# Nine small edits to the order and the buffers of a hybrid mLSTM and MLA block on one core

## The chip, the cores and the metric

The kernel runs on one core of a Trainium2 chip. The metric is the device time of one execution in microseconds (us), the median of three runs. A core has five engines that each work through an instruction queue of their own, in order: PE (TensorE, matrix products; its weight loads stand under PEld), DVE (VectorE), ACT (ScalarE), POOL (GpSimd) and SP (SyncE), which in this kernel issues all the DMAs. Semaphores hold an instruction, and with it its whole queue, until what it needs is there.

## The reference

One layer of an encoder over 2048 tokens of width 1024, all in fp32:

```python
xn = rms_norm(h, ln_mix_g);  proj = xn @ w_in
y_a = mlstm_group(q, k, v, o, gates)      # 4 heads of 128, forward and backward, in chunks of 128
y_b = mla_group(c_q, c_kv, k_rope, ...)   # 4 heads, softmax over all 2048 keys
h = h + concat(y_a, y_b) @ w_out
h = h + conv_gated_mlp(rms_norm(h))       # 2816 wide, centred convolution of 3 taps
h = h + sigmoid(rms_norm(h) @ w_ple_gate) * rms_norm(p @ w_ple_proj)
out = rms_norm(h, final_g)
```

## The kernel before, in words

Every fp32 operand of a large product is split into a high part (ACT copies it, L121) and a low part (DVE subtracts, L124), and three products of the parts are added in PSUM. Large matrices go through a Strassen-like scheme: block sums T1 to T4, B11, B21, B22 of the moving operand, sums S1 to S4 and A11 to A22 of the stationary one, seven products for a pair of column tiles.

The stages, with their time in the profiled execution:

- **Input projection** (`in_proj`, L187, 0 to 193 us). Sixteen row groups of 128 tokens. A group `st` has a product for the small columns (`nat(st, wr)`, 24 matmuls of 464), the transposes of the group before (`turn_rest`), and a product for the values (`vals`, 24 matmuls of 512). Beside them the rows' norm factors are computed (`square`: ACT squares a row tile, POOL takes the power -0.5, L144) into `rcol`. `norm_row` (L296) transposes eight columns of `rcol` on PE, and stores them to DRAM (`r_d`); `token_sums` (L398) loads them back as a broadcast (`rrow`) and forms the scaled block sums, which it stores in `xo_d` or splits at once. `norm_row` is called at groups 3 and 5, ahead of the group's product. `pair_begin` (L493) starts the next stage's first weights.
- **Pairs** (`pairs`, L503, 193 to 429 us). Twelve pairs of column tiles, seven products of 12 matmuls each. `begin` queues operands that are loaded from `xo_d` into four tiles t0 to t3 in turn; `load` splits one into place and lets the next be loaded. T3 of the first half is the first in this queue. `side(at)` runs small work between two products, and in it the generator `gates` (L870) takes a step at every second call.
- **Queries** (`queries`, L750, 429 to 495 us). Eight blocks `c` of 256 tokens: `rope(c)`, `turn(c - 1)`, `latent(c)`, with stores of the queries to `q_d`. `split_c` splits the raw latents of a block into w10 or w2 in turn. `attend_begin` (L1136) is a generator whose steps start the attention: it loads the first two query pairs (L1195, L1196) and splits the first (L1197), then scores the first tile, then takes exponentials. It is made at `c == 4`. The split query parts lie in u2 (the very first in w2).
- **Attention and mLSTM** (`attend`, L1210, 495 to 1201 us). 64 tiles (4 heads by 16), each with a written order of scores `s`, transposes `t`, exponentials `E`, value products `V`, and 13 dots. At a dot `pump` adds `rate` to a counter, and for every whole unit it takes one step of the generator `mlstm` (L979): `rate = SIDE / (64 * 13)`. The steps of `mlstm` go backward over the chunks (133 steps) and then forward (497 steps). In a forward chunk the keys are loaded from `kn_d` into w12 (`kk`, L1065, L1069), weighted (L999), and multiplied into the state (L1006); the values get a column of ones by a memset per chunk (L988); the heads' outputs `hy` are scaled by norm factors (L1125, pinned) and transposed on PE (L1130), `pause(n)` letting n dots' worth of steps go by.
- **Stream** (`stream`, L1681, 1201 to 2857 us): output projection, gated MLP, embedding gate. `opening` (L1345), stepped in the last attention tiles, loads its first weights-to-be (`yr`, from `y_d`) and their row factors (`rb`), and `Out.scale` (L1958) multiplies them (L1960).

What orders the work: the library's planner lays out each engine's queue. It takes the trace order as priority, but lets an instruction pass that it estimates to be ready earlier, so a load or a copy can stand in its queue well ahead of its place in the code (the row loads of `mlstm` at L1034 are issued at 433.23 us, amid the queries). `keep_in_program_order` pins an instruction behind all that was traced before it on its engine, and `manual_schedule` keeps an engine's whole queue in trace order, as for PE in `queries`. A tile of a tag (`self.at(tag, ...)`) takes the place of the tag's last one, and is written when all readers of that one are done.

Of the kernel before, what the change touches and what calls it, by code (L numbers as in the profile page):

```python
# [34 lines left out]
EPS = 1e-6  # L35
SB = 512
LAG_T, LAG_X, LAG_R = 1, 2, 2
SIDE = 678
KSCALE = 128.0 ** -0.5
ASCALE = 192.0 ** -0.5  # L40

# [7 lines left out]
def _f(ap):  # L49
    return ap.bitcast(F32)  # L50
# [10 lines left out]
class Block:  # L61
# [125 lines left out]
    def in_proj(self):  # L187
# [108 lines left out]
        def norm_row(blk):  # L296
            ps = self.tbank([8, P])
            nc.tensor.transpose(ps, rcol[:, 8 * blk:8 * blk + 8], self.ident)
            o = self.at(next(srot), [8, P], name="r8")
            nc.scalar.copy(o, ps)  # L300
            nc.sync.dma_start(self.r_d.rearrange("(t p) -> t p", p=P)[8 * blk:8 * blk + 8], o)
# [38 lines left out]
        for st in range(2, NT):  # L340
            if st == 4:
                pc = self.tbank([P, 36])
                nc.tensor.transpose(pc, cw, self.ident[:36, :36])
                self.taps = self.cst.tile([P, 4, 2 * NC2], F32, name="fcw")
                self.edge = self.cst.tile([P, 2 * NC2, 2], F32, name="edge")
                self.cwt = self.taps.rearrange("p a c -> p (a c)")[:, 0:36]
                nc.vector.tensor_copy(self.cwt, pc)
            if st in (3, 5):
                norm_row(st // 2 - 1)
            if st == 7:  # L350
                self.pair_load(0)
            if st + 2 < NT:
                load_x(st + 2)
            if st + 1 < NT:
                split_x(st + 1)
            rest(st, nat(st, wr, NREST))
            if st < 5:
                for q in range(4 * st - 4, 4 * st):
                    square(q)
            if st > 3:  # L360
                next(work, None)
            if st < NT - 1:
                turn_rest(st - 1)
            if st == NT - 2:
                continue
            if st == NT - 1:
                vals(st - 1)
                finish(st - 1)
                finish(st)
                turn_rest(st - 1)  # L370
            if st > 3:
                next(work, None)
            vals(st)
            if st < NT - 1:
                finish(st)
            if st > 3:
                next(work, None)
# [115 lines left out]
    def pair_begin(self):  # L493

        self.PAIRS, self.npair = (("w3", "w4"), ("x11",), ("w5", "w6"), ("w8", "w9"), ("x10",)), -1
        self.pair_load(1)
        self.begun = self.pair_prep(0)
        next(self.begun)
        yield
        next(self.begun)  # L500
        yield

    def pairs(self):  # L503
# [89 lines left out]
        class Pair:  # L593
            pass

        begin(0, ("T3", "T4", "B22"))
        gates, prev = self.gates(), None
        for i in range(12):
            blk, j = divmod(i, 6)
            then = i == 5  # L600
            s = Pair()
            s.i, s.pr, s.blk, s.ops = i, j, blk, self.ops.pop(i)
            x, s.y = [self.pfa.tile([P, SB], F32, name=t, tag=t) for t in ("fx", "fy")]
            s.z, s.spare = [self.pfb.tile([P, SB], F32, name=t, tag=t) for t in ("fz", "fs")]
            s.u = [None, None]

            def side(at):
                if i == 0 and at == 1:
                    next(self.begun)
                if i == 0 and at in (2, 3):  # L610
                    load("T3", range(2))
                if i == 0 and at in (5, 6):
                    load("T4", range(2))
                if i == 1 and at in (1, 2):
                    load("B22", range(2))
                if (1, 4) < (i, at) < (5, 0) and at % 2:
                    self.gate_bank = prev.spare if at % 2 else s.spare
                    next(gates, None)
                if i == 11:
                    self.queries_begin(at, prev.spare if at % 2 else s.spare)  # L620

            if i < 2:
                op = self.xop["B11"][0]
                nc.tensor.matmul(s.y, s.ops["A11"][0][:, 0:P], op[0], start=True, stop=True)
            prod(x, s.ops["A11"], "B11")
            nc.scalar.copy(s.y, x)
            if then:
                load("B11")
            side(1)
            prod(s.z, s.ops["S1"], "T1")  # L630
            s.p5 = self.at("t6", [P, SB], name="p5")
            nc.scalar.copy(s.p5, s.z)
            if then:
                load("T1")
            side(2)
            if prev:
                rest_y(prev)
            if i == 6:
                load("T4")
            side(3)  # L640
            prod(s.y, s.ops["S2"], "T2", True)
            s.u[0] = self.at(next(urot), [P, 2 * SB + 2], name="ug")
            nc.scalar.copy(s.u[0][:, 1 + SB:1 + 2 * SB], s.y)
            if then:
                load("T2")
            side(4)
            if i + 1 < 12:
                for _ in self.pair_prep(i + 1):
                    pass
            if i + 2 < 12:  # L650
                self.pair_load(i + 2)
            if i == 10:
                self.queries_load()
            prod(x, s.ops["A12"], "B21", True)
            first_half(s, 0, x)
            side(5)
            if prev:
                rest_z(prev)
            if i == 6:
                load("B22")  # L660
            side(6)
            if then:
                load("B21")
            prod(s.y, s.ops["S3"], "T3", True)
            s.u[1] = self.at(next(urot), [P, 2 * SB + 2], name="uv")
            add(s.u[1][:, 1 + SB:1 + 2 * SB], s.p5, s.y)
            if then:
                load("T3")
            side(7)
            if i == 4:  # L670
                begin(1, self.NAMES)
            prev = s
            if i == 4:
                assert next(gates, 0) == 0
            if i == 10:
                nc.scalar.activation(part, part, AF.Silu)
                nc.sync.dma_start(self.qk_d[7, :, :, P - 1], part)
# [72 lines left out]
    def queries(self):  # L750
# [76 lines left out]
        with self.tc.manual_schedule(engines={mybir.EngineType.PE}):  # L827
# [7 lines left out]
            for c in range(8):  # L835
# [8 lines left out]
                    kr = self.split_latent(1, ("x14", "x15"), (c - 1, c), None if c == 1 else kr)  # L844
                if c in (4, 5, 6, 7):
                    vv = self.split_latent(2, ("x10", "x11"), (c - 4,), None if c == 4 else vv)
                if 0 < c < 7:
                    split_c(c + 1)
                if c == 3:
                    self.tc.keep_in_program_order(nc.scalar.activation(self.stat(1, "warm"), self.nhalf[:, 0:1], AF.Exp))  # L850
# [1 line left out]
                    turn(c - 1)  # L852
                latent(c, 0)
                latent(c, 1)
                if c == 4:
                    self.kr2, self.krl = kr
                    att = self.attend_begin()
                    next(att)
                if c > 4:
                    next(att, None)  # L860
        self.vh, self.vl = vv
        self.last_block = lambda: turn(7)
# [7 lines left out]
    def gates(self):  # L870
# [69 lines left out]
        o = tl()  # L940
        flip(o, b)
        yield
        pt = pbank()[:, 0:16]
        nc.tensor.matmul(pt, selt, ms[:, 0:16], start=True, stop=True)
        mp, nml, so = col("mp"), col("nml"), col("so")
# [33 lines left out]
    def mlstm(self):  # L979
# [2 lines left out]
        hc = lambda n, r, j: self.cols[n].rearrange("p (r c h) -> p r c h", r=2, h=NH)[:, r, j]  # L982
        mbank = lambda s: self.pml.tile(s, F32, name="mb", tag="ml")

        def load_v(c):
            v1 = self.at(f"t{c % 2}", [P, NH, 129], name="v1")
            nc.sync.dma_start(v1[:, :, 0:P], self.v_d[c].rearrange("p (h e) -> p h e", h=NH))
            nc.vector.memset(v1[:, :, P:129], 1.0)  # L988
            return v1

        def turn_k(kn, kT):
            pk = mbank([P, NH, P])
# [62 lines left out]
        for c in range(NT):  # L1055
# [6 lines left out]
            og = self.at("t6", [P, NH, P], name="og")  # L1062
            nc.sync.dma_start(og, self.o_d[c])
            if c < NT - 1:
                kk = self.at("w12", [P, 2, NH, P], name="kk")  # L1065
                if c == 0:
                    turn_k(kk[:, 0], qk[:, 4:8, :])
                else:
                    nc.sync.dma_start(kk[:, 0], self.kn_d[c])  # L1069
# [51 lines left out]
            for h in range(NH):  # L1121
                nc.scalar.activation(hy[:, 1, h, :], hh[:, h, :], AF.Square, accum_out=ssq[:, h:h + 1])
            r4 = self.rsq(ssq, NH, 1.0 / P)
            yield from pause(2)
            a = nc.vector.tensor_tensor(hh, hh, r4.unsqueeze(2).broadcast_to([P, NH, P]), op=ALU.mult)  # L1125
            self.tc.keep_in_program_order(a)
            yield from pause(3)
# [8 lines left out]
    def attend_begin(self):  # L1136
# [4 lines left out]
        rsums = self.gt.rearrange("p a b -> p (a b)")  # L1141

        def load_q(h, pr):
            q = self.at(f"w{4 - pr % 2}", [P, 2, 256], F32R, "q_t")
            nc.sync.dma_start(_f(q), self.q_d[h, pr])
            qv[h, pr] = q

        def split_q(h, pr):

            q = qv[h, pr]  # L1150
            qs = self.at("u2" if (h, pr) != (0, 0) else "w2", [P, 2, 256], F32R, "q_s")
            self.split(_f(q[:, 0]), qs[:, 0], qs[:, 1])
            qv[h, pr] = qs[:, 0], qs[:, 1], q[:, 1]

        class Tile:
            pass
# [37 lines left out]
        self.steps = load_q, split_q, score_bank, start, soft, expo, rowsum  # L1194
        load_q(0, 0)  # L1195
        load_q(0, 1)  # L1196
        split_q(0, 0)  # L1197
        yield
        self.first = cur = start(0, 0)
# [734 lines left out]
class Out:  # L1934
# [22 lines left out]

    def scale(self, i, e):  # L1958
        a = self.b.raw[i][e][:, 4:8].rearrange("p h t -> p (h t)")
        self.nc.vector.tensor_tensor(a, a, self.rb[e], op=ALU.mult)  # L1960

    def load_x(self, i, e):
        c = self.tile(i, e)
# [372 lines left out]
```

## Time and profile before

| | us |
|---|---|
| median of 3 runs | 2856.83 |
| lowest, highest | 2855.85, 2857.14 |
| the profiled execution | 2859.16 |
| its span, first to last instruction | 2857.4 |

| engine | busy us | share of the span |
|---|---|---|
| PE | 2816.5 | 99% |
| PEld | 2363.5 | 83% |
| DVE | 2131.6 | 75% |
| ACT | 1581.6 | 55% |
| POOL | 211.1 | 7% |

The mean granted TensorE clock is 0.996. A row of the timeline has the start in us, the duration, the engine, the line (L12 is line 12 of the kernel), the operation with out<-in, the shapes, the count, and in brackets the engine's idle time before it with what ended it. A row of the waits has a waiter, what released it, the total in us, the number of times and the longest. A row of the windows has the stretch, its length, PE's busy time (and count), the mean granted clock as a share, the share of time that the DMA engines were busy, and GB/s.

### The profile page before, as it was taken

What the parts mean: (1) busy time and instruction counts of PE and PEld (TensorE: products, weight loads), DVE (VectorE), ACT (ScalarE), POOL (GpSimd) and SP (SyncE); (2) the same over time, 40 slices, a digit from 0 to 9 for tenths busy, and PEclk for the clock granted to TensorE, in tenths of its full rate; (3) what the DMA queues carried; (4) which work ended last, traced back from release to release, by engine and by line L of the source; (5) the groups of instructions that cost most, each with busy time, mean ns of one, the idle gap of its engine ahead of it and who ended that gap; (6) DMA issues with size and microseconds to landing.
All of it is one profiled execution on the core that took longest, in us unless ns stands there. A gap on an engine that the chain in (4) does not pass through costs nothing.

```text
span 2857.4 us, 39996 instructions
## 1 busy us (share of the span) xinstructions
PE 2816.5 (99%) x13932; PEld 2363.5 (83%) x13932; DVE 2131.6 (75%) x3702; ACT 1581.6 (55%) x3072; POOL 211.1 (7%) x331
## 2 busy tenths in 40 slices
PE   8999998999999999999999999999999999999998
PEld 7888887888888888888888888888888888888787
DVE  4877766777887777877778787777778767676787
ACT  6346765555566566655655556655556333254655
POOL 2100000000000000044200000000000000011012
PEclk9999999999999999999999999999999999999999
DMA  8883758554443333578735544667776757575864
GB/s 281 288 250 113 214 161 243 159 172 128 130 131 116 99 112 107 156 244 276 254 134 199 176 169 162 199 199 229 238 237 209 236 192 237 171 266 200 287 202 163
DMA packets 444531, 552.73 MB, mean 193 GB/s; under 512 B 34564, under 2 KB 296744, under 8 KB 444328
## 3 DMA queue, kind: packets, MB, share of 16 engines
q1 hardware_dynamic: 444328, 550.16, 60.1%
q8 instruction: 110, 1.80, 0.3%
q14 instruction: 93, 0.76, 0.1%
HBM read 357.45 MB, written 192.61 MB: 193 GB/s over the span
## 4 chain that ended last, share of the span: by engine, by line
PE 84%; DVE 4%; DMA 3%; ACT 2%; issue 1%; POOL 0%; SPq 0%; POOLq 0%; ACTq 0%; DVEq 0%
PE fy L1700 22%; PE fz L1700 15%; PE fx L1700 14%; PE ppv L1239 4%; PE tb L1227 3%; PE fy L541 3%; PE fz L541 2%; PE ppv L1240 2%; PE bk L1163 2%; PE bk L1165 2%; PE bk L1166 2%; PE bk L1164 2%; PE bk L1167 2%; PE fx L541 2%; PE fs L134 2%; PE mb L1101 1%
## 5 line engine op out<-in xcount | busy, mean ns | idle before, releaser
L1700 PE MATMUL fz<-op,fw 128*128 128x512 f32 x1968 | 479.3, 392 | 3.8 <-ACT fw L121 3.8
L1700 PE MATMUL fx<-op,fw 128*128 128x512 f32 x1968 | 476.0, 390 | 0.0
L1700 PE MATMUL fy<-op,fw 128*128 128x512 f32 x1968 | 475.2, 390 | 0.0
L1700 PEld LDWEIGHTS fz<-op,fw 128*128 128x128 f32 x1968 | 368.5, 188 | 81.9 <-ACT fw L121 5.0
L1700 PEld LDWEIGHTS fy<-op,fw 128*128 128x128 f32 x1968 | 368.7, 188 | 77.0 <-DVE fh L1685 0.5
L1700 PEld LDWEIGHTS fx<-op,fw 128*128 128x128 f32 x1968 | 368.4, 188 | 75.9
L121 ACT CAST pt<-tb 128x512 fp32r<-128x512 f32 x256 | 147.5, 586 | 187.9 <-PE tb L1227 187.0
L1700 PE MATMUL fy<-op,fwd 128*128 128x512 f32 (+1 forms) x984 | 238.1, 390 | 0.0
L1168 DVE TENSOR_REDUCE mx<-bk 128x1 f32<-128x512 f32 x256 | 175.4, 686 | 67.2 <-PE bk L1167 64.8
L1700 PEld LDWEIGHTS fy<-op,fwd 128*128 128x128 f32 x984 | 182.9, 188 | 37.7 <-DVE uv L1685 0.4
L124 DVE TENSOR_TENSOR pt<-tb,pt 128x512 fp32r<-128x512 f32 x256 | 173.5, 686 | 33.4 <-ACT pt L121 32.7
L1239 PE MATMUL ppv<-pt,kv 128*128 128x512 f32 x512 | 188.6, 407 | 1.0 <-DVE pt L124 1.0
L1185 ACT ACTIVATE pe<-bk,nm 128x512 f32<-128x512 f32 x256 | 174.7, 698 | 21.2 <-DVE nm L1179 21.1
L124 DVE TENSOR_TENSOR fw<-fwr,fw 128x1024 fp32r<-128x1024 f32 x124 | 150.9, 1221 | 34.0 <-ACT fw L121 32.7
L121 ACT CAST op<-opr 128x512 fp32r<-128x512 f32 x205 | 120.7, 620 | 81.2 <-DMA opr<-xo_d 16.6
L124 DVE TENSOR_TENSOR op<-opr,op 128x512 fp32r<-128x512 f32 x205 | 134.6, 690 | 25.7 <-ACT op L121 25.5
L1227 PE MATMUL tb<-ident,pe 128*128 128x128 f32 x1024 | 150.5, 273 | 1.5 <-DVE pt L124 1.3
L121 ACT CAST fw<-fwr 128x1024 fp32r<-128x1024 f32 x124 | 129.7, 1051 | 37.3 <-DVE fwr L1674 21.3
L1240 PE MATMUL ppv<-pt,kv 128*128 128x256 f32 x512 | 144.2, 282 | 0.0
L1227 PEld LDWEIGHTS tb<-ident,pe 128*128 128x128 f32 x1024 | 122.2, 141 | 20.4 <-DVE pt L124 4.1
L121 ACT CAST fw<-hraw 128x1024 fp32r<-128x1024 f32 (+1 forms) x72 | 70.2, 980 | 115.8 <-PE fx L1700 58.8
L1748 DVE SCALAR_TENSOR_TENSOR fgv<-uv,fcw,fgv 128x1024 f32<-128x1024 f32 x88 | 112.8, 1282 | 16.0 <-ACT fgv L1746 9.5
(407 smaller groups left out, 5210.1 us busy)
## 6 DMA issues: line engine op xcount, KB each, us to landing
fwr<-in_w_up SPq DMA_DIRECT2D x66, 512.0 KB
fh<-h_d SPq DMA_DIRECT2D x48, 512.0 KB
h_d<-fh SPq DMA_DIRECT2D x48, 512.0 KB
s_d<-fwr SPq DMA_DIRECT2D x44, 512.0 KB
fws<-s_d SPq DMA_DIRECT2D x44, 512.0 KB
rw<-row_d SPq DMA_DIRECT2D x32, 512.0 KB
tw_d<-tsum SPq DMA_DIRECT2D x60, 256.0 KB
opr<-tw_d SPq DMA_DIRECT2D x60, 256.0 KB
```

The source lines that it names most:

```text
L121: nc.scalar.copy(hi, src)
L124: (sub or nc.vector).tensor_tensor(lo, src, _f(hi), op=ALU.subtract)
L134: mm = lambda *a, **k: self.nc.tensor.matmul(*a, **k, skip_group_check=more)
L541: nc.tensor.matmul(out, a[:, k * P:(k + 1) * P], parts[lo], start=first, stop=lo == 1 and k == 3, skip_group_check=more)
L1163: mm(ps, ql, kh[:, ks], start=True, stop=False)
L1168: nc.vector.tensor_reduce(s.mx[:, kb:kb + 1], ps, axis=AX.X, op=ALU.max)
L1185: nc.scalar.activation(s.pe[:, kb % 2], s.banks[kb], AF.Exp, bias=s.nm, accum_out=s.rs[:, kb:kb + 1])
L1227: nc.tensor.transpose(t[:, j, :], s.p[kb][:, j * P:(j + 1) * P], self.ident)
L1239: mm(w.ps, vh[:, ks], pts[kb][:, j], start=kt == 0, stop=False, skip_group_check=True)
L1240: mm(w.ps[:, 0], vl[:, ks], pts[kb][:, j, 0], start=False, stop=kt == NT - 1, skip_group_check=True)
L1700: nc.tensor.matmul(out, a[:, k * P:(k + 1) * P], parts[lo][:, cols], start=first, stop=lo == 1 and k == last, skip_group_check=more)
L1748: nc.vector.scalar_tensor_tensor(t, u[:, tap:tap + 2 * SB], self.taps[:, tap, ct:ct + 1], t, op0=ALU.mult, op1=ALU.add)
```

## The change

1. `norm_row` is called after the group's `turn_rest`, not before its product.
2. `pair_begin` loads T3 of the first half into w12 and w13 straight away; `pairs` splits it from there, and its queue starts with T4.
3. `gates` has one more `yield` ahead of the product with `selt`, so everything from there on comes one step later.
4. `attend_begin` is made at `c == 3`; a new `yield` separates the loads from the split. The steps are: loads after block 3, split after block 4, first scores after block 5 as before, exponentials after block 6.
5. The split query parts lie in the second half of the query's own tile (w3 or w4); `split_c(7)` is traced at the end of block 5 and not in block 6.
6. The forward keys take w12 and w13 in turn.
7. The tiles of values are made once, with their ones.
8. One more pause ahead of L1125 in each of 16 chunks; `SIDE` goes from 678 to 695.
9. The two calls of `Out.scale` for the first pair are pinned.

```diff
-SIDE = 678
+SIDE = 695
...
-            if st in (3, 5):
-                norm_row(st // 2 - 1)
             if st == 7:
...
                 turn_rest(st - 1)
+            if st in (3, 5):
+                norm_row(st // 2 - 1)
...
+        self.third = [self.at(t, [P, 2, SB], name="xt3") for t in ("w12", "w13")]
+        for k in range(4):
+            self.nc.sync.dma_start(self.third[k // 2][:, k % 2], self.xo_d[0, self.NAMES.index("T3"), k])
         self.pair_load(1)
...
-        begin(0, ("T3", "T4", "B22"))
+        begin(0, ("T4", "B22"))
...
                 if i == 0 and at in (2, 3):
-                    load("T3", range(2))
+                    for k in (2 * at - 4, 2 * at - 3):
+                        self.xop["T3"][k] = self.in_place(0, "T3", k)
+                        self.split(self.third[at - 2][:, k % 2], *self.xop["T3"][k])
...
-                if 0 < c < 7:
+                if 0 < c < 6:
                     split_c(c + 1)
...
-                if c == 4:
+                if c == 3:
                     self.kr2, self.krl = kr
                     att = self.attend_begin()
-                    next(att)
-                if c > 4:
+                if c == 5:
+                    split_c(7)
+                if c > 2:
                     next(att, None)
...
         flip(o, b)
+        yield
         yield
...
+        values = [self.at(f"t{e}", [P, NH, 129], name="v1") for e in range(2)]
+        for v1 in values:
+            nc.vector.memset(v1[:, :, P:129], 1.0)
+
         def load_v(c):
-            v1 = self.at(f"t{c % 2}", [P, NH, 129], name="v1")
-            nc.sync.dma_start(v1[:, :, 0:P], self.v_d[c].rearrange("p (h e) -> p h e", h=NH))
-            nc.vector.memset(v1[:, :, P:129], 1.0)
-            return v1
+            nc.sync.dma_start(values[c % 2][:, :, 0:P], self.v_d[c].rearrange("p (h e) -> p h e", h=NH))
+            return values[c % 2]
...
-                kk = self.at("w12", [P, 2, NH, P], name="kk")
+                kk = self.at(("w12", "w13")[c % 2], [P, 2, NH, P], name="kk")
...
-            yield from pause(2)
+            yield from pause(3)
             a = nc.vector.tensor_tensor(hh, hh, r4.unsqueeze(2).broadcast_to([P, NH, P]), op=ALU.mult)
...
-            q = self.at(f"w{4 - pr % 2}", [P, 2, 256], F32R, "q_t")
-            nc.sync.dma_start(_f(q), self.q_d[h, pr])
+            q = self.at(f"w{4 - pr % 2}", [P, 4, 256], F32R, "q_t")
+            nc.sync.dma_start(_f(q[:, 0:2]), self.q_d[h, pr])
...
-            qs = self.at("u2" if (h, pr) != (0, 0) else "w2", [P, 2, 256], F32R, "q_s")
-            self.split(_f(q[:, 0]), qs[:, 0], qs[:, 1])
-            qv[h, pr] = qs[:, 0], qs[:, 1], q[:, 1]
+            self.split(_f(q[:, 0]), q[:, 2], q[:, 3])
+            qv[h, pr] = q[:, 2], q[:, 3], q[:, 1]
...
         load_q(0, 1)
+        yield
         split_q(0, 0)
...
+        if i == -8:
+            self.b.tc.keep_in_program_order(a)
```

2 lines of the change are left out of this document (1 added, 1 removed).

## The prediction, as it was put on record

> **What bounds the kernel now.** I read the page first, then who waited for whom on PE, then the granted clock by stretches, then the timeline around each long wait.
>
> ```profile
> span 2857.4 us, 39996 instructions
> PE 2816.5 (99%) x13932; PEld 2363.5 (83%) x13932; DVE 2131.6 (75%) x3702; ACT 1581.6 (55%) x3072; POOL 211.1 (7%) x331
> ```
>
> PE is busy for all but 40.9 of 2857.4 us, and no other engine passes 75%. The change takes no matmul away. So it can win only what PE stands idle, and what PE runs slowly.
>
> ```profile
> PE bk L1163 <- DVE q_s L124: 6.8, 1, 6.8
> PE tb L298 <- POOL rcol L144: 4.5, 2, 2.6
> ...
> PE mb L1130 <- DVE hy L1125: 2.2, 3, 1.0
> PE mb L1130 <- DVE v L988: 1.9, 1, 1.9
> PE fy L541 <- ACT ug L643: 1.6, 1, 1.6
> PE qpr L134 <- DVE nm L1179: 1.6, 1, 1.6
> ...
> PE fs L944 <- DVE ms L939: 0.7, 1, 0.7
> ```
>
> These are the rows of PE's waits that the edits aim at, 19.3 us together. The slow running is in the clock; the columns are the stretch, its length, PE's busy time, the granted clock as a share, the DMA share and GB/s.
>
> ```profile
> 20.00:60.00 40.00, 37.41 (x176) 1.00 0.84 266
> ...
> 70.00:78.00 8.00, 7.62 (x32) 0.79 0.82 302
> ...
> 470.00:476.70 6.70, 6.50 (x20) 0.68 0.84 246
> ...
> 696.00:704.00 8.00, 6.11 (x30) 0.79 0.45 124
> ```
>
> Behind three of the idle stretches the clock is down, and behind the one of 2.59 us (in the first row) it is not. The price can be read from the same 24 matmuls with a full clock and a low one:
>
> ```profile
> 57.20 5.30 PE L134 MATMUL bk<-wsr,xh 128*128 128x464 f32 x24
> ...
> 70.40 6.83 PE L134 MATMUL bk<-wsr,xh 128*128 128x464 f32 x24
> ```
>
> The low clock cost 6.83 - 5.30 = 1.53 us, 0.91 of the 8 x 0.21 = 1.68 that the first window gives. The same share of the others makes 0.91 x 6.7 x 0.32 = 1.95 at 470 us and 1.53 at 698 us.
>
> **The change part by part.** Each sum is against the profiled execution (2859.16 us).
>
> *The rows' factors.*
>
> ```profile
> 45.47 0.55 POOL L144 TENSOR_TENSOR rcol<-rsm,nhalf 128x1 f32<-128x1 f32 x1
> ...
> 46.07 0.27 PE L298 MATMUL tb<-ident,rcol 128*8 128x128 f32 x1 [2.59 <-POOL rcol L144]
> ...
> 51.01 0.60 PE L283 MATMUL rtp<-ident,nn 128*128 128x128 f32 x4
> ...
> 66.46 0.33 SPq L148 DMA_DIRECT2D rrow<-r_d  x1
> ...
> 69.77 0.55 POOL L144 TENSOR_TENSOR rcol<-rsm,nhalf 128x1 f32<-128x1 f32 x1
> ...
> 70.38 0.27 PE L298 MATMUL tb<-ident,rcol 128*8 128x128 f32 x1 [1.96 <-POOL rcol L144]
> ...
> 86.50 1.23 DVE L124 TENSOR_TENSOR xh<-x_t,xh 128x1024 fp32r<-128x1024 f32 x1
> ...
> 93.93 2.26 PE L134 MATMUL bk<-wsr,xh 128*128 128x464 f32 x10
> ```
>
> The transposes stand ahead of a group's product and wait for POOL's last factor. Put behind the next transposes (51.01 less the 2.59 saved, so 48.4; the other at 70.38 - 1.96 - 2.59 + 5.30 = 71.1), they come when the factors are there (46.02 and 70.32, each 0.55 after its row). This takes away 2.59 + 1.96 and the 1.53 of clock: **6.08**. Their copy and store move along, past a row-tile load and some stores in SP's queue; the first reader is the broadcast at 66.46, 15 us on, so the move costs nothing unless it is delayed to there. What is late next? PE arrives 6.1 us earlier at each group, while row loads and token sums keep their DMA time. The tightest use I find is the split of 86.50, ready at 87.7 for the product at 93.93, which would then begin at 87.8: just enough even if DVE doesn't move up at all.
>
> *T3 sooner.*
>
> ```profile
> 179.48 1.06 SPq L469 DMA_DIRECT2D fwr<-in_w_in  x2
> ...
> 197.78 8.13 SPq L518 DMA_DIRECT2D opr<-xo_d  x5
> ...
> 204.22 1.27 ACT L121 CAST op<-opr 128x512 fp32r<-128x512 f32 x2 [3.72 <-DMA opr<-xo_d]
> ...
> 206.04 3.01 PE L541 MATMUL fy<-op,fw 128*128 128x512 f32 x12 [1.58 <-ACT ug L643]
> ```
>
> ACT stands 3.72 us at the split of an operand still on its way, the copy that PE needs is queued behind it, and PE waits 1.58. With T3 loaded some 20 us earlier this goes: **1.58**. The four loads now go through SP's queue ahead of 179.48, at 0.4 to 0.6 us each some 2 us; behind them stand the weights of the next pairs, which PE wants after 193. The weights of pair 2 (179.48) lose their place in w12 and w13 and must wait until T3 is split, at about 200. Twelve matmuls take some 2.7 us, and pair 2 begins eight such products after 206.04, at 228, or 220 if all before it is won. So this costs nothing; without that cover it would cost one load, 3.86 us by the row of the queries below.
>
> *The gates a step later.* The wait of 0.7 goes (**0.68**): DVE gets two products more, 5.4 us, before PE asks. All that follows is one step later too; the generator has 14 slots for 12 steps, and its results are read after the queries, 200 us on. So nothing waits for it.
>
> *The first queries.*
>
> ```profile
> 459.42 0.60 SPq L811 DMA_DIRECT2D q_d<-qo  x1
> ...
> 465.40 1.54 SPq L1145 DMA_DIRECT2D q_t<-q_d  x2
> ...
> 470.20 0.80 PE L1163 MATMUL bk<-kv,q_s 128*128 128x512 f32 x1 [6.82 <-DVE q_s L124]
> ```
>
> The chain of waits has the load's own time:
>
> ```profile
> 465.40 3.86 DMA q_t<-q_d
> ```
>
> PE is done with block 5 at 470.20 - 6.82 = 463.38 and waits for store, load, split. The loads are behind block 4's store in SP's queue, with no wait of their own: their place in the trace holds them. Traced a block earlier they come behind the store of 459.42. So issue at 460.02, landing 3.86 later at 463.88, and to the first score the 0.94 that it takes now (469.26 to 470.20): 464.8. ACT may be at the copies of block 5 then; I add 0.2. A wait of 1.6 is left of 6.82, and the clock's 1.95 goes with the rest: 6.82 + 1.95 - 1.6 = **7.17**. If the load lands at once, 8.77; if ACT, in order, puts the split behind the copy and the load takes twice as long, 7.17 - 3.86 = 3.3. The two issues push the next stores of SP by 1.0, which nothing on PE reads.
>
> *Block 7.*
>
> ```profile
> 486.32 0.62 ACT L121 CAST cq<-qraw 128x512 fp32r<-128x512 f32 x1 [4.02 <-PE bk L1167]
> ```
>
> The split of block 7 waits for the readers of the query parts in w2, and PE's rope product waits 1.58 for it. With the parts in the query's own tile, w2 is free when block 5 is done: **1.58**.
>
> *Keys in two places, ones once.*
>
> ```profile
> 690.81 0.38 SPq L1069 DMA_DIRECT2D kk<-kn_d  x1
> ...
> 696.28 0.69 DVE L999 SCALAR_TENSOR_TENSOR kk<-kk,cols 128x512 f32<-128x512 f32 x1 [3.34 <-DMA kk<-kn_d]
> ...
> 698.30 0.66 PE L1130 MATMUL mb<-ident,hy 128*128 128x128 f32 x4 [1.89 <-DVE v L988]
> ```
>
> One place for the keys means that the load waits for the state products of the chunk before; DVE then stands 3.34 us at the weighting, and the scaling that PE's transposes need is queued behind. With two places the load is a chunk early: 1.89 and its clock 1.53, **3.42**. The memsets that go are off the path: nothing.
>
> *A pause more, and the pin.*
>
> ```profile
> 1130.75 0.44 PE L1130 MATMUL mb<-ident,hy 128*128 128x128 f32 x2 [0.80 <-DVE hy L1125]
> ...
> 1155.70 0.69 DVE L1960 TENSOR_TENSOR yr<-yr,rb 128x512 f32<-128x512 f32 x1 [2.70 <-DMA rb<-ri_d]
> ...
> 1158.58 0.66 PE L1130 MATMUL mb<-ident,hy 128*128 128x128 f32 x4 [0.97 <-DVE hy L1125]
> ...
> 1170.10 0.66 PE L1227 MATMUL tb<-ident,pe 128*128 128x128 f32 x4 [0.56 <-DVE pt L124]
> ```
>
> The transposes' group by its tile shows the chunks:
>
> ```profile
> L1130 PE MATMUL mb<-ident,hy x64: 270/273/330, 663.2 to 1159.0; 128*128 128x128 f32 x64
> ```
>
> Sixteen chunks of four, 15 periods of 31 steps in 1159.0 - 663.2 us: a step is 1.07 us. The pause moves the transposes by that much, more than the 0.80 and the 0.4 that is left of the row of 2.2: **1.19**. DVE's 2.70 us at a broadcast that hasn't landed makes the 0.97, and I put the 0.56 down to the second scaling. Pinned, the scalings come in their place some ten us later, when it has landed. But what depends on them is pushed into the last two tiles; I keep half of 1.53: **0.77**, between 1.53 and -1.5 (one more wait like the present one).
>
> The rate goes from 0.815 to 0.835 steps a dot and the generator from 630 to 646 steps, so it ends as far before tile 60 as now (5.6 steps). But every step falls elsewhere between PE's matmuls. For new waits of this kind I subtract two of 0.97: **-1.94**.
>
> Sum: 6.08 + 1.58 + 0.68 + 7.17 + 1.58 + 3.42 + 1.19 + 0.77 - 1.94 = 20.5. The profiled execution would take 2838.6. It lies 2.33 above the median of the runs shown, so I forecast **2836.3** for the median.
>
> **The rivals.**
>
> *The first queries stay late* (0.13). For it: the DMAs are busy there (a share of 0.84 from 470), and stores of queries stand ahead of the load. Against it: the load waited for nothing. Price 5.2, which would leave 2.0 of 7.17: 2841.5. It decides if the load lands after 466.
>
> *The order does not do what the edit says* (0.08): the planner puts the factors' transposes ahead of the product again. For it: the copy of 204.22 and the scaling of 1155.70 stand in their queues ahead of work that was ready. Against it: the transposes before are pinned. It costs the 6.08: 2842.4.
>
> *Short gaps cost no clock* (0.05). Then 1.53 and 1.53 were not theirs and come back elsewhere: 20.5 - 3.1 = 17.4, so 2839.4. The rows of 70 and 696 us, with gaps of 1.96 and 1.89 ahead of them, speak against it; the row of 20 us, with 2.59, speaks for it. [...]
>
> *The steps fall badly* (0.08). There is one set of transposes (L1130) in each of 16 forward chunks, and now four of them wait. If the new rate puts a wait like that of 698.30, 3.42 us with its clock, before each, the cost is 16 x 3.42 = 54.7 against 22.5 won: 2889, slower. From seven chunks on nothing is won. Against it: DVE's stall at the keys, the cause of the long one, goes. Of the 0.08, 0.03 is slower and 0.05 is within 0.2%.
>
> **How the numbers follow.** The forecast has 0.66. 0.2% of the median is 5.7 us, about what a measurement of this kernel can tell from no change; it takes 2851.1 to be faster by that. Forecast, first, second and third rival lie below it: 0.92 faster, 0.05 within, 0.03 slower. Low end: no wait left at the first scores (1.6), no new one (1.94), the pin in full (0.77), and 1 us as the runs scatter: 2831. High end: both of the first two rivals, 2836.3 + 5.2 + 6.1 = 2847.6, so 2848. Beyond are some 0.1.
>
> **What would show it.** In the waits of PE after: no row of L298 and none of fs L944; fy L541 on the ug copy gone; bk L1163 on q_s at 1 to 2 us and not 6.8; no qpr; at L1130 under 1 us. The clock is full at 64 to 72 and at about 680 to 690 us. Pairs begin near 187 us instead of 193.1, attention ends near 1181 to 1183 instead of 1201. Wrong would be: a new row of the size of those gone, above all at L1130 or at the splits of late operands (fw) before 1220 us, or PE waiting for xh in the groups after 70 us, which would say that DVE and the DMAs, not PE, set the pace there.

## The result

The changed kernel took 2846.54 us (median of 7 runs, 2842.42 to 2852.41) beside 2855.88 of the kernel before (7 runs on the same chip, 2852.84 to 2857.14): a ratio of 0.997, 95% interval 0.996 to 0.998. It is 9.3 us faster where 20.5 was forecast. The first lines of its profile:

```profile
span 2846.2 us, 39911 instructions
...
PE 2812.3 (99%) x13932; PEld 2358.7 (83%) x13932; DVE 2133.5 (75%) x3673; ACT 1579.6 (55%) x3072; POOL 212.1 (7%) x331
```

PE's waits, the view on which the prediction rests (waiting line and who released it; us in total, times, longest). The edits shift the lines: L1130 of before is L1139 here, L1163 is L1171, L1227 is L1236, L541 is L544, L1700 is L1709. Of the tiles, `nn` holds the finished rows of q and kv that PE transposes, `pe` a tile's exponentials and `pt` their split transposes, `hy` the scaled outputs of the heads, `ug` and `uv` what the pairs write, `fy` a bank of PSUM with PE's sums.

```profile
PE fz L1709 <- ACT fw L121: 3.8, 3, 2.4
PE tb L1236 <- DVE pt L124: 3.1, 5, 1.7
PE mb L1139 <- DVE hy L1134: 2.7, 3, 1.6
PE bk L1171 <- DVE q_t L124: 2.6, 1, 2.6
...
PE rtp L283 <- DVE nn L274: 1.6, 2, 1.2
PE bk L1171 <- ACT pe L1193: 1.5, 2, 0.9
...
PE fy L544 <- DVE uv L562: 0.9, 1, 0.9
PE fy L1709 <- DVE uv L1694: 0.9, 1, 0.9
PE fy L544 <- ACT fy L631: 0.5, 1, 0.5
```

Of the rows that the edits aimed at, those for rcol, ug, v, nm and ms are gone, the first queries' is smaller (2.6 and not 6.8), and the one for hy grew, from 2.2 to 2.7. There are new ones, for nn, pe, uv and fy, and the row of pt grew from 1.3 to 3.1. The clock says the same. After the first scores it is still low; near 71 and 698 us it is full now:

```profile
70.00:78.00 8.00, 8.00 (x41) 1.00 0.88 300
459.97:466.67 6.70, 6.70 (x25) 0.75 0.71 231
688.00:700.00 12.00, 11.94 (x77) 1.00 0.30 106
```

The profiled execution of after is 11.2 us shorter than that of before (2857.4 - 2846.2). Where that came from is told below in five stretches, which are cut at the same products of PE in every kernel.

### The profile page after: what moved, and what is told of

Its sections match the earlier page's. It is cut to its first block, busy times and chain, and to the rows that moved or that the text cites. A ratio compares the mean times of both kernels' runs of the same rounds, so it can differ in the third digit from the quotient of the medians.

```text
span 2846.2 us, 39911 instructions
## 1 busy us (share of the span) xinstructions
PE 2812.3 (99%) x13932; PEld 2358.7 (83%) x13932; DVE 2133.5 (75%) x3673; ACT 1579.6 (55%) x3072; POOL 212.1 (7%) x331
## 4 chain that ended last, share of the span: by engine, by line
PE 83%; DMA 6%; DVE 6%; ACT 2%; issue 2%; SPq 1%; POOL 0%; ACTq 0%; POOLq 0%; DVEq 0%
PE fy L1709 21%; PE fz L1709 14%; PE fx L1709 14%; PE ppv L1248 3%; PE fy L544 3%; PE tb L1236 3%; PE bk L134 2%; PE fx L544 2%; PE fz L544 2%; PE bk L1171 2%; PE ppv L1249 2%; PE bk L1173 2%; PE bk L1172 2%; PE bk L1175 2%; PE bk L1174 2%
## 5 line engine op out<-in xcount | busy, mean ns | idle before, releaser
L1709 PE MATMUL fz<-op,fw 128*128 128x512 f32 x1968 | 479.6, 392 | 4.3 <-ACT fw L121 3.8
L1709 PE MATMUL fx<-op,fw 128*128 128x512 f32 x1968 | 475.9, 390 | 0.0
L1709 PE MATMUL fy<-op,fw 128*128 128x512 f32 x1968 | 474.9, 390 | 0.0
L1709 PEld LDWEIGHTS fz<-op,fw 128*128 128x128 f32 x1968 | 367.7, 188 | 83.3 <-ACT fw L121 5.0
L1709 PEld LDWEIGHTS fy<-op,fw 128*128 128x128 f32 x1968 | 368.6, 188 | 76.8 <-DVE fh L1694 0.2
L1709 PEld LDWEIGHTS fx<-op,fw 128*128 128x128 f32 x1968 | 368.1, 188 | 76.1
L1709 PE MATMUL fy<-op,fwd 128*128 128x512 f32 (+1 forms) x984 | 238.5, 390 | 0.9 <-DVE uv L1694 0.9
L1709 PEld LDWEIGHTS fy<-op,fwd 128*128 128x128 f32 x984 | 183.2, 188 | 39.1 <-DVE uv L1694 1.3
L1236 PE MATMUL tb<-ident,pe 128*128 128x128 f32 x1024 | 150.8, 273 | 3.2 <-DVE pt L124 3.1
L1236 PEld LDWEIGHTS tb<-ident,pe 128*128 128x128 f32 x1024 | 122.5, 140 | 23.3 <-DVE pt L124 5.3
```

The costliest lines, as they stand in the source:

```text
L1236: nc.tensor.transpose(t[:, j, :], s.p[kb][:, j * P:(j + 1) * P], self.ident)
L1709: nc.tensor.matmul(out, a[:, k * P:(k + 1) * P], parts[lo][:, cols], start=first, stop=lo == 1 and k == last, skip_group_check=more)
```

## The experiments

Each kernel ran in five rounds with the kernel before on the same chip, unless said; its median there is given as a ratio to that of before. All profiles were cut in the same way, by the starts of PE's products: A to the first product of the pairs (L541 or L624 of before), B on to the last one of L541, C on to the tenth on the scores' line L1163, D on to the last value product (L1239), E to the end. Where one row of a group shows it, it can be read off directly, here C's beginning and A's end in after:

```profile
L544 PE MATMUL fz<-op,fw x288: 388/389/478, 188.0 to 420.3; 128*128 128x512 f32 x144
L544 PE MATMUL fy<-op,fwd x144: 387/389/497, 208.5 to 423.0; 128*128 128x512 f32 x144
```

| stretch, us | without the edit in question | with it |
|---|---|---|
| A, rows' factors | 191.1 (6 profiles, 190.0 to 193.1) | 188.7 (11, 188.0 to 190.3) |
| B, T3 and gates | 234.2 (11, 233.9 to 236.1) | 235.0 (7, 234.9 to 236.0) |
| C, queries | 68.1 (6, 67.7 to 68.4) | 61.7 (5, 59.6 to 62.9); two blocks sooner 58.4 (7, 58.3 to 58.5) |
| D, attention's edits, old queries | 702.0 (4, 701.5 to 703.5) | all of them 703.5 (1) |
| D, attention's edits, new queries | 698.2 (3, 698.1 to 699.0) | all of them 701.4 (3, 701.3 to 702.9) |
| E, no edit | 1654.5 to 1659.8 (18) | |

The first profile of before has 193.1, 235.95, 68.1, 703.5 and 1656.75. The profile of after has 188.0, 235.0, 62.2, 702.9 and 1658.1. The two ranges of A touch, so its difference is the least sure one: of the eleven, the six with T3's old load have a median of 189.45. B's ranges overlap too.

**One part at a time, on the kernel before.** Rows' factors alone:

```diff
-            if st in (3, 5):
-                norm_row(st // 2 - 1)
...
             if st < NT - 1:
                 turn_rest(st - 1)
+            if st in (3, 5):
+                norm_row(st // 2 - 1)
```

> The kernel before with only the transposes of the rows' factors moved behind the next group's transposes. Theory (PE comes sooner, but DVE's finishing of the q/kv rows does not): the two waits of 4.5 us for rcol go, the clock's 1.5 us too, and one or two new waits of 0.4 to 1.2 us stand at the rtp transposes; the pairs begin 4.5 us sooner than before, time 2851.4. Rival (the prediction as it stood, nothing late next): pairs begin 6.1 us sooner, no new wait, 2849.8. Second rival (the loss in the changed kernel came from another edit): as the first rival.

Measured: 2852.73 beside 2853.13, ratio 0.9995 (0.9986 to 1.0003). In its waits and timeline rcol is gone and nn has come:

```profile
PE rtp L283 <- DVE nn L274: 2.2, 2, 1.8
...
84.03 0.63 PE L283 MATMUL rtp<-ident,nn 128*128 128x128 f32 x4 [1.78 <-DVE nn L274]
```

So the theory's mechanism holds. Its size doesn't: the pairs begin at 189.7, 3.4 us sooner than in the first profile where the theory had 4.5, and 1.4 sooner than in the median of the table. In the time next to nothing is left.

Keys in two places alone (`self.at("w12", ...)` to `self.at(("w12", "w13")[c % 2], ...)`):

> The kernel before with only the second place for the second pass's keys. Theory (the free place lets the weighting of the keys move up with the load and stand on it): the wait for v and its slow clock near 698 us go (3.4 us), but the first key load is issued some 40 us sooner than at 657, DVE's idle time for the key loads rises from 7.6 us to over 11, and PE has a new wait of 1 to 2 us behind it somewhere in the first passes; net 1 to 2.5, time 2853.4 to 2854.9. Rival (prediction): 3.4 won and DVE's idle time for the keys near zero, 2852.5.

Measured: 2854.1, ratio 1.0005 (0.9997 to 1.0014). The wait for v is gone, DVE's idle time for the key loads rose from 7.6 to 10.3 us, and PE's waits for hy rose too. One of them, the second row here, stands at 693 us, where the wait for v is in the kernels without this edit (691 to 696 us):

```profile
PE mb L1130 <- DVE hy L1125: 3.8, 5, 1.4
...
PE mb L1087 <- DVE hy L1131: 2.1, 1, 2.1
```

The queries' part alone (the edits to attend_begin's loads and splits, and to the loop over c that calls them):

> The kernel before with only the queries' part (load a block sooner, query parts in the query's own tile, block 7 split after it). Theory (the store queue ahead of the load holds it, and a gap of over 2 us still lowers the clock): the wait before the first score falls from 6.8 to 2.6 us, not to 1.6, the clock stays low for 3.4 us after it, block 7's wait goes but the first tile's exponentials cost about 0.9; net 5.9 us at the end of the queries, time 2850.0. Prediction: 8.75, 2847.1. Rival (the later attention is disturbed by it): under 4 us, over 2852.

Measured: 2843.71, ratio 0.9963 (0.995 to 0.9976), 9.4 us. C is 61.7, so 6.4 is won there. The wait is 1.8, where the theory had 2.6, and the clock is low for 3.4 us after it, as the theory said. D is 699.0 and so shorter too, by 3.0, which neither had. The size of the whole was the prediction's, but not where it comes from.

T3 sooner and the gates' second yield alone:

> The kernel before with T3 loaded sooner and the gates a step later, nothing else. Theory (the wait of 1.6 us was mostly one execution's, and the edits bring waits of their own): no wait for ug, but one of 0.5 to 0.7 us for fy's copy and one of 0.9 for uv; the stretch from the first product of the pairs to their last takes as long as in the unchanged kernels, 234 to 236 us, or 1 us more; time within 1.5 us of the kernel before. Prediction: the stretch is 2.3 us shorter than the 235.95 of the first profile, 233.7, and the time 2.3 less.

Measured: 2857.35, ratio 1.001 (1.0001 to 1.002): slower by 3, if anything. B is 234.9, beside a median of 234.2 without these edits. The two waits that came:

```profile
PE fy L544 <- DVE uv L562: 0.9, 1, 0.9
...
PE fy L544 <- ACT fy L631: 0.7, 1, 0.7
```

Every edit but the queries' (the changed kernel with that one undone):

> The changed kernel with the queries' part as it was before: every other edit, without that one. Theory (nothing but the queries' part gains): within 1.5 us of the kernel before, 2851.5 to 2854.5 where that takes 2853; the rcol waits are replaced by waits for nn, a new wait stands behind the key loads. Prediction: the other terms sum to 11.7, so 2841.4. Rival (half of each term is real): 2847.

Measured: 2853.42, ratio 0.9998 (0.999 to 1.0007). Seven edits, for which 11.8 us were forecast, are together worth nothing that can be measured. In the profile A is 188.7 and 2.4 shorter than the median without, B is 235.9 and D 703.5, 1.7 and 1.5 longer: what the rows' factors win, the others lose.

**The kernel before once more, for one profile and one time.**

> The kernel before, unchanged: a second profile of it. Theory (some of the waits that the prediction priced belong to one execution and not to the code): the wait of 1.6 us at L541 for T3's split is under 0.5 us, the clock isn't halved near 71 us, the waits for rcol are 3 to 4 us and not 4.5, so that the pairs begin about 3 us sooner than in the first profile; the wait before the first score is 6.5 to 7.1 us with 6.8 us at half the clock again; span 2852 to 2855. Rival (the first profile is typical): the waits of 1.6, 4.5 and 1.9 us and the low clock near 71 and 698 us come again, each within 0.3 us.

Measured: 2851.0; the span is 2849.2, 8.2 us shorter than in the first profile, with the same instructions. Its waits:

```profile
PE bk L1163 <- DVE q_s L124: 6.9, 1, 6.9
...
PE mb L1130 <- DVE v L988: 2.0, 1, 2.0
PE tb L298 <- POOL rcol L144: 1.7, 1, 1.7
...
PE fy L541 <- ACT ug L643: 0.6, 1, 0.6
```

and its clock in the stretches that the prediction priced:

```profile
60.00:78.00 18.00, 17.89 (x86) 1.00 0.84 294
460.00:470.30 10.30, 3.93 (x9) 0.67 0.93 279
688.00:704.00 16.00, 13.96 (x85) 1.00 0.51 177
```

The wait at the scores came again, with its slow clock, and so did the wait for v, at full clock. Of the 4.5 us for rcol 1.7 are left, of T3's 1.6 there are 0.6, and the clock is full near 71 and 698 us. So the direction is the theory's; the span and rcol's waits are smaller than it had them (2852 to 2855, 3 to 4), and v is as the rival had it.

The other profiles with the same code say how much of each belongs to the code:

- T3's old load: of eleven profiles one, the first, has 1.6 us for ug, one has 1.1, the others have 0 to 0.6.
- The wait for v with the old queries and keys: 1.7 to 2.0 us in all four profiles, with the slow clock in the first (0.79 from 696 to 704 us) and at full clock in the second (1.00 from 688 to 704).
- The rows' factors in their old place: of six profiles all have the first wait, with 1.7 to 2.6 us; four have the second with 1.6 to 2.0, and two have 0 and 0.3. Slow clock follows near 70 us in the first and in that of T3 and the gates alone. The latter has the price of the prediction once more, 6.82 us for the same 24 matmuls:

```profile
69.24 0.27 PE L298 MATMUL tb<-ident,rcol 128*8 128x128 f32 x1 [1.92 <-POOL rcol L144]
69.27 6.82 PE L134 MATMUL bk<-wsr,xh 128*128 128x464 f32 x24
```

**Whether the pace took the gain back.** The changed kernel with SIDE = 678 and pause(2) again:

> The changed kernel with the old pace of the side work (the old SIDE and the old pause). Rival (the new pace is what gave the gain back): the waits of 0.2 to 1.7 us between 560 and 1150 us go and the time falls by 2.5, to 2844.0. Theory (they come from the key loads and the queries' part, not from the pace): the same kind of waits at other places, time within 1 us of the changed kernel, 2846.5, with the hy transposes' waits some 0.5 to 1 us larger.

Measured: 2845.34, ratio 0.9972 (0.9961 to 0.9982), and D is 702.3, beside 702.9 in after: the pace isn't it.

**What is next in line.** In the changed kernel, finish(st) ahead of the second next(work):

> The changed kernel with the finishing of the q and kv rows put ahead of the second step of the token sums on DVE. Theory (after the row factors moved, DVE's finishing is the next in line): the rtp waits of 1.6 us go and the pairs begin 1.2 to 1.6 us sooner; 2845. Rival (the projection is held by its loads and by DVE's whole work there): the wait goes to a product that waits for the split of a row tile, pairs begin as before, 2846.5.

Measured: 2845.91, ratio 0.9973 (0.9963 to 0.9983). The wait changed its releaser and grew, from 1.6 in after to 3.5 in the two rows below, and A is 190.2, longer than after's 188.0:

```profile
PE rtp L283 <- DVE nn L270: 2.1, 3, 1.2
...
PE rtp L283 <- DVE nn L269: 1.4, 1, 1.4
```

The theory is wrong. The rival is right that the pairs begin no sooner, but the wait stays at the transposes (L283) and doesn't go to the split of a row tile: DVE is late there with whatever it does last for them.

The weighting of the keys in the second pass kept in program order, in the changed kernel:

```diff
+            if r == 0:
+                self.tc.keep_in_program_order(a)
```

> The changed kernel with the weighting of the second pass's keys held to its place in the program's order on DVE. Theory (with two places the weighting goes up with its load and DVE stands on it): DVE's idle time for the key loads falls from 13.7 us to under 4, the PE wait of 1.7 us near 614 goes, and attention from its ninth score to its last value product takes 700 to 701.5 us in place of 702.9; time 2845. Rival (attention's small waits come from alignment and not from this stall): the idle time falls, the stretch stays at 702 to 704 us, 2846.5.

Measured: 2846.3, ratio 0.9972 (0.9961 to 0.9984). No idle time of DVE is put down to the key loads any more, the 1.7 us near 614 are gone, as the theory had it, but D is 702.0, which is the rival's. The rows that the theory rested on, in after, show a real wait, and without it D is no shorter than that of the other kernels with these edits (701.3 to 702.9):

```profile
612.18 1.30 DVE L1008 SCALAR_TENSOR_TENSOR kk<-kk,cols 128x512 f32<-128x512 f32 x2 [1.80 <-DMA kk<-kn_d]
...
614.13 0.66 PE L1236 MATMUL tb<-ident,pe 128*128 128x128 f32 x4 [1.72 <-DVE pt L124]
```

**The queries another block sooner.** attend_begin is made at c == 2, so that the loads come after block 2, and takes no step at c == 3; the split stays after block 4. This is done on the queries' part alone and on the changed kernel:

> The kernel before with the queries' part alone, and the first loads of the queries another block sooner. Theory (the load's place in SP's queue sets the first score): the wait of 1.8 us before the first score goes, and with it the 3.4 us at half the clock; 3 us below the run with the queries' part alone, 2840.7. Rival (the DMA engines are full there, and the load lands no sooner): the wait stays over 1 us, 2843.7. Second rival: the two loads push the stores of the next block back and a wait of 1 to 2 us comes at a later block, 2842 to 2844.

> The changed kernel with the first loads of the queries another block sooner. Theory (as in the run of the queries' part alone with the same step): the wait of 2.6 us before the first score goes, and with it the half clock; 3.5 to 4 us less than the changed kernel, 2842.7. Rival (the wait goes, something else of the two blocks takes it over): 2845 to 2847.

Measured: 2842.18, ratio 0.9959 (0.9946 to 0.9971), and 2844.76, ratio 0.9967 (0.9955 to 0.998). The loads are issued at 450.58, the split is done at 456.52 + 0.41, PE comes at 460.76 and neither waits nor runs slowly (the clock is 1.00 from 457 to 465 us):

```profile
450.58 1.52 SPq L1147 DMA_DIRECT2D q_t<-q_d  x2
...
456.52 0.41 DVE L124 TENSOR_TENSOR q_t<-q_t 128x256 fp32r<-128x256 f32 x1
...
460.76 0.40 PE L1164 MATMUL bk<-kv,q_t 128*128 128x512 f32 x1
```

C is 58.3 and 58.4: 9.7 us less than before. D is 698.1 in the first and 701.4 in the second.

**The version that beats both.** The kernel before with the queries two blocks sooner and the rows' factors moved, and nothing else:

> The kernel before with the queries' part two blocks sooner and the rows' factors turned a group later, and no other edit: the version that should beat both kernels. Theory (the rows' move is worth 1 to 1.6 us, the other edits nothing or less): 2840.7. Prediction's price for the rows: 6.1 below the run without them, 2836. Rival (the rows are worth nothing in the time): 2842.2.

Measured: 2841.07 (2838.53 to 2842.76), ratio 0.9953 (0.9941 to 0.9966): 12.9 us under the kernel before on its chip, and 3.7 under the changed kernel with the queries sooner, which ran beside it. How much of the 12.9 the rows' factors give isn't shown: without them it was 12.0, and the two intervals overlap. Each edit inside attention put onto it:

> The kernel with the queries two blocks sooner and the rows' factors moved, and the keys in two places. Stretch from the ninth score to the last value product, 698.2 us without the edit. Theory (the keys' edit is the one that costs, through DVE standing on a key load that it meets earlier): 700 to 701.5 us, DVE's idle time for the keys up from 7.6 to over 10, time 2843. Rival (another edit): 697.5 to 699, 2841.1. Prediction's sign (3.4 won): under 697.

> The kernel with the queries two blocks sooner and the rows' factors moved, and the first scaling pinned. Stretch from the ninth score to the last value product, 698.2 us without the edit. Theory (the pin does nothing but move one wait of about 1 us): 697.5 to 699, 2841.1. Rival (the pin costs): 700 or more, with a wait for hy over 2 us near the end of attention, 2843.

> The kernel with the queries two blocks sooner and the rows' factors moved, and the new pace (SIDE 695 and three steps' pause). Stretch from the ninth score to the last value product, 698.2 us without the edit. Theory (the pace costs nothing by itself, as its undoing in the changed kernel gained 0.6): 697.5 to 699.5, 2841.1. Rival (the pace costs): over 700.5, with new waits at the pt splits, 2843.5.

> The kernel with the queries two blocks sooner and the rows' factors moved, and the ones beside the values written once. Stretch from the ninth score to the last value product, 698.2 us without the edit. Theory (two places for the whole of the passes, 29 memsets of 0.06 us less, nothing on the path): 697.5 to 699, 2841.1. Rival (fixing the places lets the value loads go earlier and DVE or SP meet them): over 700, 2843.

Measured: keys 2841.71 (0.9951, 0.9937 to 0.9964), pin 2839.63 (0.9945, 0.9932 to 0.9957), pace 2840.66 (0.9952, 0.994 to 0.9965), ones 2839.52 (0.9947, 0.9934 to 0.9959); D is 698.8, 698.5, 699.0 and 697.9. None costs or gains what can be told from 698.2, and the theory of the keys is wrong here (DVE's idle time for the key loads is 6.4 us and not over 10). All four together, in the run with the queries sooner, have 701.4. Why they cost 3 us together and 1.1 as a sum (0.5 + 0.2 + 0.8 - 0.4) stays open.

## Why the prediction was wrong

The direction was right and the time lies in the range; the gain was forecast at more than twice its size. By the stretches:

| step | forecast | first profile above the others | measured | lost in the step |
|---|---|---|---|---|
| rows' factors (A) | 6.1 | 2.0 | 2.4 | 1.7 |
| T3, gates (B) | 2.3 | 1.8 | -0.8 | 1.3 |
| queries, block 7 (C) | 8.75 | 0 | 6.4 | 2.35 |
| the same edits, in attention (D) | 0 | 0 | 3.8 | -3.8 |
| keys, ones, pause, pin, new waits (D) | 3.4 | 1.5 | -3.2 | 5.1 |
| sum | 20.5 | 5.3 | 8.6 | 6.6 |

The second column is the first profile of before less the median in the table of the stretches; the third is that median less the one with the edit, in D 702.0 - 698.2 for the queries and 698.2 - 701.4 for the other four edits. The sum of 8.6 stands beside 9.3 in the times. So by this table the gain is the queries' part, and the other seven edits together give a little less than nothing.

- **The failed step is the one that took each row of PE's waits, and the slow clock behind it, as what the code costs each time and what the edit would win.** Two things were wrong in it. A part of the price belongs to that one execution: T3's 1.58, the clock's 1.53 at 698 us, and some of the waits and the clock at the rows' factors, which come and go from profile to profile; by the stretches 5.3 of 20.5. And where the wait did go, another came behind it: the rows' factors won 2.4 of 6.1, T3 and the gates lost 0.8, and the four edits inside attention, forecast at +3.4, lost 3.2. For all new waits together the sum had 1.94.
- **The 2.33.** The prediction took the 2.33 by which the first profile lies above the median off the forecast once more, as if they lay outside the waits that it had counted as won. By the stretches they lie inside them.
- **Rows' factors.** "What is late next" was looked for at the split of a row tile (86.50). Nearer by was nn: in before DVE finished it at 86.00 + 0.48, and PE's transposes took it at 88.02, 1.5 us later. In after PE came 6.7 us sooner (82.48 less its wait of 1.17) and DVE 4.2, so PE waits for nn:

```profile
86.00 0.48 DVE L274 SCALAR_TENSOR_TENSOR nn<-rs,rsr,gn 128x256 f32<-128x256 f32 x1
...
88.02 0.60 PE L283 MATMUL rtp<-ident,nn 128*128 128x128 f32 x4
```

```profile
81.85 0.48 DVE L274 SCALAR_TENSOR_TENSOR nn<-rs,rsr,gn 128x256 f32<-128x256 f32 x1
...
82.48 0.63 PE L283 MATMUL rtp<-ident,nn 128*128 128x128 f32 x4 [1.17 <-DVE nn L274]
```

- **T3 and the gates.** The waits for ug and ms went, as forecast; 0.94 for uv and 0.53 for fy came with these edits, behind DVE's work on uv and ACT's copy into fy. "So this costs nothing" didn't look there.
- **First queries.** The loads were issued at 454.53, 5 us sooner than by the old order (465.40 less the 6.0 by which PE was ahead there). But that is 2.8 us ahead of PE, which was free at 459.97 - 2.63 = 457.34, where the prediction had 3.4 (463.38 - 460.02): SP stood in the four stores of L829.

```profile
449.50 4.30 SPq L829 DMA_DIRECT2D q_d<-qso  x4
...
454.53 1.55 SPq L1154 DMA_DIRECT2D q_t<-q_d  x2
...
458.96 0.41 ACT L121 CAST q_t<-q_t 128x256 fp32r<-128x256 f32 x1
```

  The other part is the 0.2 us for ACT. The chain of waits in after (start, us, what):

```profile
451.62 2.17 SPq L829
...
453.84 4.07 DMA q_d<-qo
...
457.99 1.09 ACT qo L814 x2
459.07 0.30 ACT q_t L121
...
459.97 0.77 PE bk L1171
```

  It doesn't end in the load. Behind SP's four stores is the store of a query copy, 4.07 us long; until it is done, ACT may not write the next copy into that place; and the split of the queries stands in order behind two such copies. The trace of after doesn't tell when the first load landed. In before it took 3.86 us; by that it landed at about 458.4 here (an estimate), 0.6 ahead of the split. So of the 1.0 us by which the wait (2.63) is longer than the forecast 1.6, about 0.55 is the later issue and 0.4 is ACT's order. The prediction had named the split behind the copy, with a load that takes twice as long, at 3.3 and left it; the first half came, the second didn't. And the clock's 1.95, which was to go with the rest, stayed as 1.7 (6.70 x 0.25, by the window above): a gap of 2.6 was followed by half rate as well. A block sooner, the load's landing frees the split (ACT waits for it until 454.60), it stands ahead of the copies, and nothing is left for PE to wait for. The 1.58 of block 7 went; 0.94 for an exponential came at 483.61.
- **The queries in attention.** That D gets 3.8 us shorter with the queries' part was in no term. PE's waits there fall by 2.1 us: the wait for v goes, and at its place PE waits 0.5 to 1.5 us for hy. Why the rest of the 3.8 goes is open.
- **Keys, pause, pin.** "With two places the load is a chunk early" holds for the load and not for DVE. The weighting moves up in DVE's queue with its load, and DVE stands at the key loads longer (7.6 us before, 10.3 with the keys alone, 13.7 in after) until it is held to its place. This too depends on what is around it: with the keys' edit put onto the queries two blocks sooner, DVE's idle time there is 6.4. In the run with the keys alone 2.1 us for hy came where 1.9 for v went. The wait for v goes in the runs with the queries alone too, where that edit isn't made, so the 3.42 was not the keys' to win. The pin left a wait of its kind: DVE stands 3.40 us at the same broadcast, and PE 1.57 for hy (before: 2.70 and 0.97).

```profile
1144.07 0.69 DVE L1969 TENSOR_TENSOR yr<-yr,rb 128x512 f32<-128x512 f32 x1 [3.40 <-DMA rb<-ri_d]
...
1146.21 0.68 DVE L1134 TENSOR_TENSOR hy<-hy,rsr 128x512 f32<-128x512 f32 x1
...
1146.94 0.65 PE L1139 MATMUL mb<-ident,hy 128*128 128x128 f32 x4 [1.57 <-DVE hy L1134]
```

- **The rivals.** The first queries stayed late, by 1 us of wait and 1.7 of clock where the rival had 5.2, and only in part by the load that it named. The order did what the edit says: no kernel with the rows' factors moved has a wait for rcol. "Short gaps cost no clock" had 0.05 and is right for some executions and wrong for others (below). The steps did not fall as badly as that rival had it: three waits for hy, 2.7 us together. That the time lies inside the range is luck in part, as the unforecast 3.8 of the queries made up for what the other edits in attention lost.

## What to carry to other kernels

A wait in one profile is a cost of the code only if a second profile of the same kernel shows it too; take that second one, or another kernel with the same code there, ahead of adding small waits up. Of a list of small waits, expect the one to pay whose cause is a chain (store, load, split) with its own place in a queue, and whose size is far above the scatter; for the others look for the operand that is ready with the least to spare behind the one that you free. When the one real gain is found, carry it through (here a block more) and leave the rest out.

## What the runs showed of the hardware

In the traces of before and after the clock is full but for pieces at half of it (0.50 in a window inside one), which last 3.41 or 6.83 us, but for the piece at each kernel's end. Before has 6.83 us from 467.41 us on, and 3.41 from 71.46, from 699.52 and from 2679.25 on; after has 3.41 from 459.89 and from 2668.31 on. (In a window a piece's length is twice the lost share: 2 x 0.33 x 10.3 us gives 6.8 in the second profile of before.)

The length of the gap ahead doesn't settle it alone. In these two traces, without their first 20 and last 30 us, PE has six gaps of 1.8 to 2.8 us. Five of them (1.89, 1.96 and 2.34 in before, 2.37 and 2.63 in after) have a piece of 3.41 us, which starts between 0.1 us ahead of the gap's end and 1.9 behind it; the sixth, of 2.59 (rcol in before), has none, and nor have the shorter ones, of 1.72 and less. The gap of 6.82 ahead of the first scores in before has the piece of 6.83, which starts 2.8 us ahead of the gap's end; in the second profile a gap of 6.9 there has 6.8. In the other runs, gaps of 1.5 (finish(st) first) and 1.6 (the weighting in order) ahead of the first scores went by at full clock (1.00 from 457 to 466 us and from 455 to 465), and behind one of 1.78 (nn, rows alone) the 24 matmuls of 512 took 5.71 us, beside 5.74 ahead of it. The wait for v had the slow clock with 1.89 us in the first profile of before, and not with 2.0 in the second. What decides it the traces don't show.

Stretch E, which no edit touches, took 1654.5 to 1659.8 us in 18 profiles, 5 us apart: more than half of what the change is worth.
